# Moving elementwise work from GpSimd to VectorE in a two-layer attention kernel

## The chip, the core and the metric

The kernel runs on one core of a Trainium2 chip. A core has five engines, each with its own in-order instruction queue: TensorE (PE; its weight loads are listed as PEld), VectorE (DVE), ScalarE (ACT), GpSimd (POOL) and SyncE (SP), whose queue issues the transfers (DMAs). Engines wait for each other by semaphores. The metric is the device time of one execution in microseconds (us).

## What is computed

One step of a backbone with two layers over 256 context tokens and 1024 latent tokens, width 1024. Layer 0 mixes tokens by differential attention, layer 1 by multi-head latent attention. Each layer is a gated mixer between two normalisations, with shift, scale and gate computed from a conditioning vector. Cut to what matters here:

```
for i in range(2):
    hc = rmsnorm(x_ctx, g_pre[i]) * (1 + sc_c) + sh_c      # and hl from x_lat
    # i == 0: q, k, v, gate = h @ w_in; rope on q, k of latents; cached k, v appended
    #         w = softmax(q0 k0) - lam * softmax(q1 k1); o = w @ v per head
    #         o = rmsnorm(o, g_sub) * 0.8 * silu(gate)
    # i == 1: latent projections; k, v = c_kv @ w_kvb; o = softmax(q k) @ v * silu(gate)
    x_ctx = x_ctx + gt_c * rmsnorm(oc @ w_out[i], g_post[i])   # x_lat alike
```

Everything is float32. The outputs are both token streams and the new key/value states of the context tokens.

## The kernel before

**Products in three parts.** TensorE works on a reduced float32 form (fp32r). So each operand is kept as a high part, rounded to that form, and a low part, the operand minus its high part; a product is three matmuls, high x high, low x high, high x low (`mm3`, L327 to L329). Somebody has to make the low parts by a subtraction:

- for the weights, `weights` (L304): a piece of a weight matrix is loaded to a staging tile `wst` (three buffers, L317), ACT casts it to `wh` (L319), and L320 subtracts to `wl`. L320 runs on POOL, unless the caller hands `lo_engs`: with `self.LO` (L101) pieces alternate between POOL and DVE. This is so in the output projections (L971), layer 1's input projections (L1017, L1130) and the first head's key, query and value weights of layer 1 (L1193, L1215, L1235, with DVE first). Layer 0's value and gate weights (L499) and the later heads of layer 1 use POOL alone. A twin for rotated layouts, `weights_x` (L347), uses POOL at L365.
- for the normalised input, `norm_pair_to_hT` (L280): PE transposes a chunk (L290), ACT applies scale and shift into `hfull` (L297), DVE casts the high part `hh` (L298), and L299 makes the low part `hl`, in layer 0 by DVE for odd chunks and by POOL for even ones, in layer 1 by DVE for six of the eight (`HL`, L90).

**Tokens** are handled in five pairs of 128-token tiles, four of the latents and one of the context (`CTXP`).

**Layer 0** first computes the norms and the first value product, then query and key projections, then goes through the heads (`l0_heads`, L820). For each unit of 128 queries and one head, PE computes scores S into one of two PSUM buffers (L603), DVE takes their maxima (L605, L612, L613) and the bias (L614), ACT the exponentials (L617, L619), which frees S; DVE combines the two softmaxes (L639 to L648); PE transposes the weights (L671), ACT and DVE split them into high and low parts (L673, L674), and PE multiplies with the values (`l0_values`, L678). Between the steps of the units, a feeder (`Feeder`, L31) inserts pieces of the remaining projections, so that PE has work while the softmax chain runs. At the end of a pair, `l0_values` squares and sums the output (L701), takes the reciprocal root (`rstd`, L248: a multiply-add L251 and a power L253 on POOL), forms the row factor f (L706), scales y by it (L707) and stores y (L708).

**Gating.** `y_chunk` (L743) loads stored y and gate, multiplies them (L757), and PE transposes the product for the output projection (L768).

**Output projection** (`out_items`, L929): products per pair, squares summed by ACT (L954), small sums (L965, L966), then `residual` (L974): the root's argument (L980, DVE), the power (L983, POOL), and for either tile the scaled product (L987, DVE), its sum with x (L989, POOL), and z times the row factor plus x (L995, DVE; where z isn't scaled yet, L991 and L993). After layer 0 the result goes through `norm_pair` (L256: squares on ACT, a small sum L266, `rstd`, scaling L270) and `norm_pair_to_hT`; after layer 1 it is stored (L1692, L1693) and the kernel ends.

**Layer 1** has its projections (`l1_items`, L1042, with `row_norm` L1033 through `rstd`) and its heads (`l1_heads`, L1332), with scores (L1277 to L1281), bias (L1293), exponentials (L1295) and normalisation (L1302). L1407 and L1408 split layer 1's output again, the low part on POOL.

The order of instructions in each queue comes from a scheduler in the framework, which works from priorities and its own estimates; only the PE order of the first stage is written out by hand (L1510). A change of an engine can therefore move other instructions in the queues.

Of the kernel before, what the change touches and what calls it, by code (L numbers as in the profile page):

```python
# [12 lines left out]
ALU = mybir.AluOpType  # L13
# [4 lines left out]
P = 128  # L18
D = 1024
KC = 8  # L20
H = 8
EPS = 1e-6
# [55 lines left out]
def f32(ap):  # L78
    return ap.bitcast(F32)


class K:
# [16 lines left out]
    def __init__(self, tc, I, O):  # L99
        self.tc = tc  # L100
        self.LO = [tc.nc.gpsimd, tc.nc.vector]  # L101
        self.nc = tc.nc
        self.I = I
        self.O = O
        self.n = 0
# [142 lines left out]
    def rstd(self, pool, ss, n, width=1, tag="rs"):  # L248
        nc = self.nc
        v = self.t(pool, [P, width], tag + "v")  # L250
        nc.gpsimd.tensor_scalar(out=v, in0=ss, scalar1=1.0 / n, scalar2=EPS, op0=ALU.mult, op1=ALU.add)  # L251
        r = self.t(pool, [P, width], tag)
        nc.gpsimd.tensor_tensor(out=r, in0=v, in1=self.mhalf[:, 0:width], op=ALU.pow)  # L253
        return r

    def norm_pair(self, xs, pool, sp):  # L256

        nc = self.nc
        n = len(xs[0])
# [5 lines left out]
        if n == 2:  # L265
            nc.gpsimd.tensor_tensor(out=ss[:, 0, :], in0=ss[:, 0, :], in1=ss[:, 1, :], op=ALU.add)  # L266
        r = self.rstd(sp, ss[:, 0, :], D, 2)
# [12 lines left out]
    def norm_pair_to_hT(self, xs, l, pair, big, pool, ps, pstag):  # L280
# [4 lines left out]
        for kk in range(0, KC, 2):  # L285
# [6 lines left out]
            for j in range(2):  # L292
                k = kk + j
                a = self.ada[l][:, 1, k, cond:cond + 1]
                s = self.ada[l][:, 0, k, cond:cond + 1]
                full = self.t(pool, [P, 256], "hfull", bufs=3 - l)
                nc.scalar.activation(full, pt[:, j, :], AF.Identity, scale=a, bias=s)  # L297
                nc.vector.tensor_copy(hh[:, k, :], full)  # L298
                (nc.vector if k in (self.HL if l else (1, 3, 5, 7)) else nc.gpsimd).tensor_tensor(out=hl[:, k, :], in0=full, in1=f32(hh[:, k, :]),  # L299
                                                              op=ALU.subtract)  # L300
            yield kk


    def weights(self, W, cols, kb=2, lo_engs=None, ks=None):  # L304

# [4 lines left out]
        for k0 in range(*(ks or (0, nk)), kb):  # L310
# [8 lines left out]
            nc.scalar.copy(wh, st)  # L319
            (lo_engs or [nc.gpsimd])[k0 // kb % len(lo_engs or [0])].tensor_tensor(out=wl, in0=st, in1=f32(wh), op=ALU.subtract)  # L320
            out += [(wh[:, j, :], wl[:, j, :]) for j in range(kn)]
# [356 lines left out]
    def l0_values(self, u, rz, vh, vl, feed):  # L678
# [25 lines left out]
        for i in range(2):  # L704
            f = self.t(c.st, [P, 1], "of")
            nc.gpsimd.tensor_tensor(out=f, in0=r[:, i:i + 1], in1=rz[i], op=ALU.mult)  # L706
            nc.gpsimd.tensor_scalar(out=y[:, i, :], in0=y[:, i, :], scalar1=f, scalar2=None, op0=ALU.mult)  # L707
        nc.sync.dma_start(self.ydram[pr].rearrange("(t p) n -> p t n", p=P)[:, :, h * P:(h + 1) * P], y)  # L708
# [34 lines left out]
    def y_chunk(self, pr, kk, late=None, alt=False):  # L743
# [12 lines left out]

        nc.gpsimd.tensor_tensor(out=y, in0=y, in1=g, op=ALU.mult)  # L757
        yield 1
# [170 lines left out]
    def out_items(self, l, groups, yT, zp, pool, sp, pj, gps, after):  # L929
# [7 lines left out]
        def item(n, prs):  # L937
            def gen(ws):
                for pr in prs:
# [6 lines left out]
                    for tiles in [(0,), (1,)] if l and n == 3 and pr == NPAIR - 1 else [(0, 1)]:  # L946
# [16 lines left out]
                        if n == 2:  # L963
                            for j in (1, 2):
                                nc.gpsimd.tensor_tensor(out=ss[:, 0, :], in0=ss[:, 0, :], in1=ss[:, j, :], op=ALU.add)  # L965
                            nc.gpsimd.tensor_scalar(out=ss[:, 0, :], in0=ss[:, 0, :], scalar1=1.0 / D,  # L966
                                                    scalar2=EPS, op0=ALU.mult, op1=ALU.add)
                        after(n, pr, tiles, (zs[pr], ps, ss, gp))
                    if pr == prs[-2]:
                        yield None  # L970
            return lambda: self.weights(W, [(n * 256, 256)], lo_engs=self.LO), gen  # L971
        return [item(n, prs) for prs in groups for n in range(4)]

    def residual(self, zz, tiles, x0, xt, gp, pool, sp):  # L974
# [9 lines left out]
        for i in tiles:  # L984
# [3 lines left out]
                                           op0=ALU.mult, op1=ALU.mult)  # L988
            nc.gpsimd.tensor_tensor(out=xt[:, i, :], in0=xt[:, i, :], in1=tmp, op=ALU.add)  # L989
            if scaled is None:  # L990
                nc.vector.scalar_tensor_tensor(out=z[:, i, :], in0=z[:, i, :], scalar=ri, in1=gp[0],  # L991
                                               op0=ALU.mult, op1=ALU.mult)
                nc.gpsimd.tensor_tensor(out=z[:, i, :], in0=z[:, i, :], in1=x0[i], op=ALU.add)  # L993
            else:
# [4 lines left out]
    def l1_tok_item(self, cols, pj, evac, before):  # L999
# [4 lines left out]
        def gen(ws):  # L1004
            for pr in self.ORD1:
# [9 lines left out]
                if pr == self.ORD1[-2]:  # L1015
                    yield None
        return lambda: self.weights(W, cols, lo_engs=self.LO), gen  # L1017

# [23 lines left out]
    def l1_items(self, c1, c2, later, switch):  # L1042
# [68 lines left out]
        def gate_item(h):  # L1111
            def gen(ws):
                yield None
                for s in range(0, NPAIR, 2):
# [13 lines left out]
                    for j in range(n):  # L1128
                        nc.sync.dma_start(self.gTd[h][s + j], g[:, j, :])
            return lambda: self.weights(W, [(704 + h * P, P)], kb=4, lo_engs=self.LO), gen  # L1130

# [57 lines left out]
    def l1_kn(self, h, out):  # L1189

        nc, c, m, I = self.nc, self.c, self.m, self.I
        Wk = I["mla_w_kvb"][0].rearrange("(kc p) n -> p kc n", p=P)
        wk = self.weights(Wk, [(h * 256, P)], lo_engs=self.LO[::-1] if h == 0 else None)  # L1193
        yield 1
# [16 lines left out]
    def l1_qn(self, h, out):  # L1211

        nc, c, m, I = self.nc, self.c, self.m, self.I
        Wq = I["mla_w_qb"][0].rearrange("(kc p) n -> p kc n", p=P)
        wq = self.weights(Wq, [(h * 192, P)], lo_engs=self.LO[::-1] if h == 0 else None)  # L1215
        yield 1
# [14 lines left out]
    def l1_v(self, h, out):  # L1231

        nc, c, m, I = self.nc, self.c, self.m, self.I
        Wk = I["mla_w_kvb"][0].rearrange("(kc p) n -> p kc n", p=P)
        wv = self.weights(Wk, [((h + j) * 256 + P, P) for j in range(2)], lo_engs=self.LO[::-1] if h == 0 else None)  # L1235
        yield 1
# [513 lines left out]
```

## Time and profile before

| what | value |
|---|---|
| median of 3 runs | 1993.41 us (1992.21 to 1994.4) |
| the profiled execution, its time | 1997.65 us |
| the profiled execution, its span | 1995.8 us |
| busy: PE, DVE, ACT, POOL | 1911.7, 1248.4, 963.9, 498.9 us |
| mean granted TensorE clock | 0.989 |

The span runs from the first to the last instruction of the profiled execution. A group of instructions is named by its line in the kernel, its engine, its operation and out<-in; then come the count, the busy time, the mean duration in ns, and the idle time of the engine just before with what ended it. A line "X <- Y: total, times, longest" says that instruction X's engine stood still until Y had finished.

### The profile page before, as it was taken

How to read it: one execution, taken by the hardware profiler on the slowest of the kernel's cores; microseconds unless marked ns; L12 is line 12 of the kernel's file. 1: busy time of each engine (PE TensorE's matmuls, PEld its weight loads, DVE VectorE, ACT ScalarE, POOL GpSimd, SP SyncE). 2: the span in 40 equal slices, each digit the busy share in tenths (PEclk: the TensorE clock that was granted, in tenths of full speed). 3: DMA queues.
4: the chain of work that ended last, by engine and by line, in shares of the span. 5: the costliest groups of instructions: out<-in, count | busy, mean ns of one | idle time of the engine just before them, and what ended most of it. 6: DMA issues, size and time to landing. Idle time of an engine off the chain costs nothing.

```text
span 1995.8 us, 36154 instructions
## 1 busy us (share of the span) xinstructions
PE 1911.7 (96%) x13468; PEld 1721.9 (86%) x13468; DVE 1248.4 (63%) x2461; ACT 963.9 (48%) x2409; POOL 498.9 (25%) x693
## 2 busy tenths in 40 slices
PE   6999999999999999999998999999999999999998
PEld 5788888798989787988898999889899999998998
DVE  4644446788878786888427533446667767777413
ACT  4422123667666665666435533335445554455421
POOL 3354443213121212224334442100000000004214
PEclk9999999999999999999998999999999999999999
DMA  8555544544455454455624312442110111113412
GB/s 307 170 169 175 188 157 137 157 138 132 128 147 162 129 165 127 133 148 180 194 98 135 97 51 62 145 135 60 42 36 28 47 39 50 38 38 96 160 56 106
DMA packets 225009, 237.66 MB, mean 119 GB/s; under 512 B 25313, under 2 KB 192577, under 8 KB 224705
## 3 DMA queue, kind: packets, MB, share of 16 engines
q1 hardware_dynamic: 224672, 235.29, 38.3%
q8 instruction: 107, 1.75, 0.4%
q14 instruction: 70, 0.57, 0.1%
q10 hardware_dynamic: 160, 0.05, 0.0%
HBM read 160.48 MB, written 74.78 MB: 118 GB/s over the span
## 4 chain that ended last, share of the span: by engine, by line
PE 43%; DVE 5%; POOL 3%; ACT 2%; issue 2%; DMA 2%; SPq 0%; POOLq 0%; ACTq 0%; DVEq 0%
PE pj L327 7%; PE pj L329 7%; PE pj L328 7%; PE tp L671 3%; PE tp L327 3%; PE tp L328 3%; PE tp L329 3%; PE S L1280 1%; PE S L1281 1%; PE S L1278 1%; PE S L1279 1%; PE S L1277 1%; PE S L603 1%; DVE ptl L674 1%; DMA yst<-yTd 1%
## 5 line engine op out<-in xcount | busy, mean ns | idle before, releaser
L327 PE MATMUL pj<-wh,hh 128*128 128x256 f32 (+1 forms) x1264 | 369.4, 292 | 6.6 <-DVE ptl L674 3.5
L328 PE MATMUL pj<-wl,hh 128*128 128x256 f32 (+1 forms) x1264 | 359.1, 284 | 6.1 <-DVE wl L320 3.7
L329 PE MATMUL pj<-wh,hl 128*128 128x256 f32 (+1 forms) x1264 | 358.8, 284 | 3.4 <-POOL hl L299 1.7
L320 POOL TENSOR_TENSOR wl<-wst,wh 128x512 fp32r<-128x512 f32 (+3 forms) x95 | 110.7, 1173 | 655.1 <-ACT wh L319 608.9
L327 PEld LDWEIGHTS pj<-wh,hh 128*128 128x128 f32 x1264 | 241.7, 191 | 11.7 <-DVE ptl L674 4.1
L328 PEld LDWEIGHTS pj<-wl,hh 128*128 128x128 f32 x1264 | 242.2, 192 | 8.3 <-DVE wl L320 4.1
L329 PEld LDWEIGHTS pj<-wh,hl 128*128 128x128 f32 x1264 | 241.7, 191 | 6.5 <-POOL hl L299 3.1
L329 PE MATMUL pj<-hh,wl 128*128 128x512 f32 (+1 forms) x512 | 188.5, 368 | 1.0 <-POOL wl L365 0.9
L327 PE MATMUL pj<-hh,wh 128*128 128x512 f32 (+1 forms) x512 | 188.3, 368 | 0.0
L328 PE MATMUL pj<-hl,wh 128*128 128x512 f32 (+1 forms) x512 | 187.8, 367 | 0.0
L605 DVE TENSOR_REDUCE mA<-S 128x1 f32<-128x1024 f32 x128 | 155.4, 1219 | 46.8 <-PE S L603 45.9
L617 ACT ACTIVATE e<-S,bias 128x1024 f32<-128x1024 f32 x128 | 142.9, 1117 | 81.6 <-DVE bias L614 81.4
L603 PE MATMUL S<-kl,q 128*128 128x512 f32 x512 | 150.4, 414 | 5.5 <-ACT e L617 5.1
L673 ACT CAST pth<-tp 128x512 fp32r<-128x512 f32 (+1 forms) x208 | 98.4, 511 | 83.0 <-PE tp L671 81.9
L673 ACT CAST pth<-pj 128x512 fp32r<-128x512 f32 (+1 forms) x192 | 98.4, 519 | 73.4 <-PE pj L671 70.8
L674 DVE TENSOR_TENSOR ptl<-tp,pth 128x512 fp32r<-128x512 f32 (+1 forms) x208 | 115.1, 580 | 14.1 <-ACT pth L673 13.3
L648 DVE SCALAR_TENSOR_TENSOR e<-e,cf,e 128x512 f32<-128x512 f32 (+1 forms) x192 | 121.4, 674 | 1.1
L674 DVE TENSOR_TENSOR ptl<-pj,pth 128x512 fp32r<-128x512 f32 (+1 forms) x192 | 113.0, 592 | 12.1 <-ACT pth L673 11.5
L329 PEld LDWEIGHTS pj<-hh,wl 128*128 128x128 f32 x512 | 96.3, 188 | 20.9 <-POOL wl L365 3.9
L328 PEld LDWEIGHTS pj<-hl,wh 128*128 128x128 f32 x512 | 96.3, 188 | 16.9
L319 ACT CAST wh<-wst 128x512 fp32r<-128x512 f32 (+3 forms) x136 | 76.7, 574 | 70.1 <-issue 24.9
L603 PEld LDWEIGHTS S<-kl,q 128*128 128x128 f32 x512 | 88.8, 192 | 25.1 <-ACT e L617 8.1
(323 smaller groups left out, 5247.7 us busy)
## 6 DMA issues: line engine op xcount, KB each, us to landing
q<-qsd SPq DMA_DIRECT2D x320, 64.0 KB, 2.1
wst<-in_da_w_in_dram SPq DMA_DIRECT2D x64, 256.0 KB, 3.5
kl<-ksd SPq DMA_DIRECT2D x64, 192.0 KB, 3.7
wst<-in_w_out_dram SPq DMA_DIRECT2D x48, 256.0 KB, 2.9
ast<-in_w_ada_dram SPq DMA_DIRECT2D x8, 1024.0 KB, 6.3
wh<-in_w_ada_dram SPq DMA_DIRECT2D x32, 256.0 KB, 4.2
wl<-in_w_ada_dram SPq DMA_DIRECT2D x32, 256.0 KB, 5.1
vdh<-s SPq DMA_DIRECT2D x24, 256.0 KB, 2.1
```

The source lines that it names most:

```text
L319: nc.scalar.copy(wh, st)
L320: (lo_engs or [nc.gpsimd])[k0 // kb % len(lo_engs or [0])].tensor_tensor(out=wl, in0=st, in1=f32(wh), op=ALU.subtract)
L327: nc.tensor.matmul(out, a[0], b[0], start=first, stop=False)
L328: nc.tensor.matmul(out, a[0], b[1], start=False, stop=False)
L329: nc.tensor.matmul(out, a[1], b[0], start=False, stop=last)
L603: nc.tensor.matmul(S[:, so:so + 512], st(cc, o), kl[cc][:, so:so + 512], start=(o == 0), stop=(o == 1))
L605: nc.vector.reduce_max(out=mA[:, cc:cc + 1], in_=S, axis=AX.X)
L617: nc.scalar.activation(u.es[cc][:, 0:1024], A[cc], AF.Exp, bias=bias[:, cc:cc + 1], scale=0.125, accum_out=u.zA[:, cc:cc + 1])
L648: nc.vector.scalar_tensor_tensor(out=w[:, sl], in0=w[:, sl], scalar=cf, in1=e0[:, sl], op0=ALU.mult, op1=ALU.add)
L671: nc.tensor.transpose(tp[:, j, :], u.e[:, (c0 + j) * P:(c0 + j + 1) * P], self.ident)
L673: nc.scalar.copy(hi, tp[:, 0:cn, :])
L674: nc.vector.tensor_tensor(out=u.ptl[g][:, 0:cn, u.i * P:(u.i + 1) * P], in0=tp[:, 0:cn, :], in1=f32(hi), op=ALU.subtract)
```

## The change

VectorE does several kinds of small and middling elementwise work that GpSimd did: all low parts of weights in `weights` (the choice by `lo_engs` is gone), all low parts in `norm_pair_to_hT`, the multiply-add in `rstd` (the power stays on GpSimd), the scaling of y (two GpSimd instructions per tile become one VectorE instruction with two row factors), the gating of y, the residual additions, and the small sums of squares. `weights_x`, the rotation of q, the power, and L1408 stay on GpSimd.

```
@@ rstd
-        nc.gpsimd.tensor_scalar(out=v, in0=ss, scalar1=1.0 / n, scalar2=EPS, op0=ALU.mult, op1=ALU.add)
+        nc.vector.tensor_scalar(out=v, in0=ss, scalar1=1.0 / n, scalar2=EPS, op0=ALU.mult, op1=ALU.add)
@@ norm_pair
-            nc.gpsimd.tensor_tensor(out=ss[:, 0, :], in0=ss[:, 0, :], in1=ss[:, 1, :], op=ALU.add)
+            nc.vector.tensor_tensor(out=ss[:, 0, :], in0=ss[:, 0, :], in1=ss[:, 1, :], op=ALU.add)
@@ norm_pair_to_hT
-                (nc.vector if k in (self.HL if l else (1, 3, 5, 7)) else nc.gpsimd).tensor_tensor(out=hl[:, k, :], in0=full, in1=f32(hh[:, k, :]),
-                                                              op=ALU.subtract)
+                nc.vector.tensor_tensor(out=hl[:, k, :], in0=full, in1=f32(hh[:, k, :]), op=ALU.subtract)
@@ weights
-            (lo_engs or [nc.gpsimd])[k0 // kb % len(lo_engs or [0])].tensor_tensor(out=wl, in0=st, in1=f32(wh), op=ALU.subtract)
+            nc.vector.tensor_tensor(out=wl, in0=st, in1=f32(wh), op=ALU.subtract)
@@ l0_values
         for i in range(2):
-            f = self.t(c.st, [P, 1], "of")
-            nc.gpsimd.tensor_tensor(out=f, in0=r[:, i:i + 1], in1=rz[i], op=ALU.mult)
-            nc.gpsimd.tensor_scalar(out=y[:, i, :], in0=y[:, i, :], scalar1=f, scalar2=None, op0=ALU.mult)
+            nc.vector.tensor_scalar(out=y[:, i, :], in0=y[:, i, :], scalar1=r[:, i:i + 1], scalar2=rz[i],
+                                    op0=ALU.mult, op1=ALU.mult)
@@ y_chunk
-        nc.gpsimd.tensor_tensor(out=y, in0=y, in1=g, op=ALU.mult)
+        nc.vector.tensor_tensor(out=y, in0=y, in1=g, op=ALU.mult)
@@ out_items
-                                nc.gpsimd.tensor_tensor(out=ss[:, 0, :], in0=ss[:, 0, :], in1=ss[:, j, :], op=ALU.add)
-                            nc.gpsimd.tensor_scalar(out=ss[:, 0, :], in0=ss[:, 0, :], scalar1=1.0 / D,
+                                nc.vector.tensor_tensor(out=ss[:, 0, :], in0=ss[:, 0, :], in1=ss[:, j, :], op=ALU.add)
+                            nc.vector.tensor_scalar(out=ss[:, 0, :], in0=ss[:, 0, :], scalar1=1.0 / D,
                                                     scalar2=EPS, op0=ALU.mult, op1=ALU.add)
@@ residual
-            nc.gpsimd.tensor_tensor(out=xt[:, i, :], in0=xt[:, i, :], in1=tmp, op=ALU.add)
+            nc.vector.tensor_tensor(out=xt[:, i, :], in0=xt[:, i, :], in1=tmp, op=ALU.add)
...
-                nc.gpsimd.tensor_tensor(out=z[:, i, :], in0=z[:, i, :], in1=x0[i], op=ALU.add)
+                nc.vector.tensor_tensor(out=z[:, i, :], in0=z[:, i, :], in1=x0[i], op=ALU.add)
```

The callers of `weights` lose their `lo_engs` argument.

More of the change, by code (lines that the diff above doesn't have):

```diff
@@ L100, in __init__ @@
         self.tc = tc
-        self.LO = [tc.nc.gpsimd, tc.nc.vector]
         self.nc = tc.nc
@@ L298, in norm_pair_to_hT, with weights @@
                 nc.vector.tensor_copy(hh[:, k, :], full)
-                (nc.vector if k in (self.HL if l else (1, 3, 5, 7)) else nc.gpsimd).tensor_tensor(out=hl[:, k, :], in0=full, in1=f32(hh[:, k, :]),
-                                                              op=ALU.subtract)
+                nc.vector.tensor_tensor(out=hl[:, k, :], in0=full, in1=f32(hh[:, k, :]), op=ALU.subtract)
             yield kk
-    def weights(self, W, cols, kb=2, lo_engs=None, ks=None):
+    def weights(self, W, cols, kb=2, ks=None):
         nc, wp = self.nc, self.wp
@@ L970, in gen @@
                         yield None
-            return lambda: self.weights(W, [(n * 256, 256)], lo_engs=self.LO), gen
+            return lambda: self.weights(W, [(n * 256, 256)]), gen
         return [item(n, prs) for prs in groups for n in range(4)]
@@ L1016, in gen @@
                     yield None
-        return lambda: self.weights(W, cols, lo_engs=self.LO), gen
+        return lambda: self.weights(W, cols), gen
     def split_T(self, ps, pstag, srcs, out, nb):
@@ L1129, in gen @@
                         nc.sync.dma_start(self.gTd[h][s + j], g[:, j, :])
-            return lambda: self.weights(W, [(704 + h * P, P)], kb=4, lo_engs=self.LO), gen
+            return lambda: self.weights(W, [(704 + h * P, P)], kb=4), gen
         Wq = I["mla_w_qb"][0].rearrange("(kc p) n -> p kc n", p=P)
@@ L1192, in l1_kn @@
         Wk = I["mla_w_kvb"][0].rearrange("(kc p) n -> p kc n", p=P)
-        wk = self.weights(Wk, [(h * 256, P)], lo_engs=self.LO[::-1] if h == 0 else None)
+        wk = self.weights(Wk, [(h * 256, P)])
         yield 1
@@ L1214, in l1_qn @@
         Wq = I["mla_w_qb"][0].rearrange("(kc p) n -> p kc n", p=P)
-        wq = self.weights(Wq, [(h * 192, P)], lo_engs=self.LO[::-1] if h == 0 else None)
+        wq = self.weights(Wq, [(h * 192, P)])
         yield 1
@@ L1234, in l1_v @@
         Wk = I["mla_w_kvb"][0].rearrange("(kc p) n -> p kc n", p=P)
-        wv = self.weights(Wk, [((h + j) * 256 + P, P) for j in range(2)], lo_engs=self.LO[::-1] if h == 0 else None)
+        wv = self.weights(Wk, [((h + j) * 256 + P, P) for j in range(2)])
         yield 1
```

## The prediction

> **What bounds the kernel now.** I read the page first, then a windows view whose cuts I chose at the stages of the code: 0 to 100 us layer 0's first norms and products, 320 to 950 layer 0's attention, 950 to 1160 its output projection with residual and norm, 1350 to 1850 layer 1's attention, then the last projection. Its columns are the window, its length, and busy time (instructions) of PE, PEld, DVE, ACT, POOL.
>
> ```profile
> span 1995.8 us, 36154 instructions
> ...
> PE 1911.7 (96%) x13468; PEld 1721.9 (86%) x13468; DVE 1248.4 (63%) x2461; ACT 963.9 (48%) x2409; POOL 498.9 (25%) x693
> ...
> 0.00:100.00 100.00, 80.49 (x569) 66.18 (x570) 54.98 (x119) 42.30 (x81) 35.53 (x51) 0.97 0.72 239
> ...
> 320.00:950.00 630.00, 607.82 (x4383) 538.49 (x4382) 511.67 (x1003) 408.12 (x1068) 150.08 (x267) 0.99 0.50 147
> 950.00:1160.00 210.00, 190.82 (x1524) 182.44 (x1524) 109.03 (x194) 103.45 (x276) 86.05 (x117) 0.96 0.40 128
> ...
> 1350.00:1850.00 500.00, 492.27 (x3509) 449.54 (x3508) 357.50 (x823) 253.54 (x618) 39.53 (x49) 1.00 0.16 47
> 1850.00:1996.00 146.00, 134.35 (x1119) 132.28 (x1117) 46.95 (x83) 44.84 (x141) 40.51 (x54) 0.98 0.32 110
> ```
>
> PE is busy 96% of the span: POOL's time is nowhere the bound by itself, and emptying POOL buys only those moments in which PE waits for a chain with a POOL step in it. All PE idle time together is 1995.8 - 1911.7 = 84 us. The engine that gets the work is at 63% over the whole, but at 511.67/630 = 81% in layer 0's attention. So that stage decides, and I asked who waits for whom there (microseconds in total, times, longest):
>
> ```profile
> ACT e L617 <- DVE bias L614: 81.4, 52, 4.5
> ...
> DVE mA L605 <- PE S L603: 45.9, 43, 3.0
> DVE Z L639 <- ACT e L619: 45.7, 27, 3.4
> ...
> PEld S L603 <- ACT e L617: 8.1, 10, 3.0
> ...
> 455.42 0.14 DVE L614 SCALAR_TENSOR_TENSOR bias<-m,negl 128x2 f32<-128x2 f32 x1
> ...
> 455.60 1.12 ACT L617 ACTIVATE e<-S,bias 128x1024 f32<-128x1024 f32 x1 [1.47 <-DVE bias L614]
> ...
> 456.87 1.18 PE L603 MATMUL S<-kl,q 128*128 128x512 f32 x4
> ```
>
> There is a loop: scores S (L603), their maximum (L605, L612), the bias (L614), the exponential (L617), which frees the S buffer for the next scores. The exponential waited for DVE's bias in 52 of 64 units. In the timeline rows it ends at 455.60 + 1.12 = 456.72 and PE starts the next scores at 456.87: no slack at this place. What is put in DVE's queue ahead of L614 can reach PE.
>
> **The change part by part.** What leaves POOL, and what the same shapes cost on DVE (busy us, mean ns):
>
> ```profile
> L320 POOL TENSOR_TENSOR wl<-wst,wh 128x512 fp32r<-128x512 f32 x71 | 94.0, 1331 | 228.9 <-ACT wh L319 184.5 <-PE tp L671 44.1 <-DMA wst<-in_da_w_in_dram 0.4
> L707 POOL TENSOR_SCALAR y<-y,of 128x128 f32<-128x128 f32 x80 | 51.5, 656 | 0.0
> ...
> L253 POOL TENSOR_TENSOR ors<-orsv,mhalf 128x2 f32<-128x2 f32 x40 | 29.0, 724 | 3.3
> L299 POOL TENSOR_TENSOR hl<-hfull,hh 128x256 fp32r<-128x256 f32 x30 | 22.8, 760 | 52.6 <-DVE hh L298 52.6
> ...
> L989 POOL TENSOR_TENSOR x<-x,ztmp 128x256 f32<-128x256 f32 x10 | 14.4, 1438 | 6.0 <-DVE ztmp L987 6.0
> ...
> L1293 DVE TENSOR_SCALAR bias<-mm 128x1 f32<-128x1 f32 x80 | 11.9, 149 | 1.4
> ...
> L639 DVE TENSOR_TENSOR Z<-Z,zA 128x2 f32<-128x2 f32 x64 | 9.9, 155 | 45.7 <-ACT e L619 45.7
> ...
> L1302 DVE TENSOR_SCALAR e<-e,rz 128x256 f32<-128x256 f32 x16 | 6.3, 393 | 0.5
> ...
> L429 DVE TENSOR_TENSOR r<-r,m 128x512 f32<-128x512 f32 x8 | 5.5, 684 | 0.0
> ...
> L1167 DVE TENSOR_TENSOR qa<-qa,gTh 128x256 f32<-128x256 f32 x8 | 3.3, 416 | 0.0
> ```
>
> A subtract or multiply of 128x512 costs 0.684 us on DVE (L429, both inputs in SBUF), of 128x256 0.416 (L1167), a small sum 0.155 (L639). The scaling of y, 128x128 with two per-row factors, has no row on DVE: L1293 (one column, 0.149) and L1302 (256 columns, 0.393) bound it; 128 columns lie halfway, so I take 0.27, and the product of the two factors (L706) vanishes into it. [...]
>
> *Layer 0's attention.* Counts in the stage, by the windows view of each line (here DVE busy, POOL busy, or POOL alone):
>
> ```profile
> 320.00:950.00 630.00, 0.00 (x0) 30.91 (x24) 0.99 0.50 147
> ...
> 1350.00:1850.00 500.00, 1.40 (x2) 21.66 (x27) 1.00 0.16 47
> ...
> 320.00:950.00 630.00, 49.11 (x76) 0.99 0.50 147
> ...
> 320.00:950.00 630.00, 20.07 (x15) 0.99 0.50 147
> ```
>
> In order: L320 in this stage and in layer 1's attention, L707, L757. DVE gains 24 x 0.684 = 16.4 (weights' low parts), 76 x 0.27 = 20.5 (y), 15 x 0.684 = 10.3 (gating) and 38 x 0.155 = 5.9 (L251, one for two of L707): 53 us. Something comes back, because DVE and POOL get in each other's way:
>
> ```profile
> L614 DVE SCALAR_TENSOR_TENSOR bias<-m,negl x64: 143/151/1316, 323.4 to 949.4; 128x2 f32<-128x2 f32 x64
> ...
> L614 DVE SCALAR_TENSOR_TENSOR bias<-m,negl 128x2 f32<-128x2 f32 x64 | 14.2, 221 | 0.2
> ...
> 1046.55 1.26 POOL L320 TENSOR_TENSOR wl<-wst,wh 128x512 fp32r<-128x512 f32 x1 [0.30 <-ACT wh L319]
> ...
> 1046.58 2.05 DVE L995 SCALAR_TENSOR_TENSOR z<-z,rs,x 128x768 f32<-128x768 f32 x1
> ```
>
> L614 (minimum, median, maximum in ns) is a 0.151 us instruction that once took 1.316; against its median it loses 64 x (0.221 - 0.151) = 4.5 us. I put the three small instructions around the bias (L613, L614, L643) at three times this, 13, an estimate. DVE goes to 511.67 + 53 - 13 = 552 of 630, 88%. How much reaches PE? The quoted idle times, 45.9 in 43 waits and 45.7 in 27, are gaps of 1.3 us between busy stretches; an added instruction pushes its stretch to the next gap, about every second stretch holds a bias, and where it does, PE's slack is between nothing (the rows at 455 us) and some microseconds. Bounds: nothing of the 53 reaches PE, or all. I take a quarter of it, +13, and a third of the 13 given back, -4 (it sits on the loop itself): **+9**, from -4 to +40.
>
> *Start.* By the code 20 of the 30 L299 belong to layer 0 (four chunks of five pairs), at the start; DVE then makes both low parts of a pair in turn, 0.416 each, where POOL took 0.760 and held DVE up meanwhile. Output stage: residual and norm are chains with three or four POOL steps.
>
> ```profile
> PE xt L290 <- ACT hfull L297: 9.8, 5, 3.4
> ...
> PE pj L768 <- POOL xt L757: 3.3, 1, 3.3
> ...
> PE pj L329 <- POOL hl L299: 1.7, 6, 0.3
> ```
>
> At the start at most the 1.7 us of PE's wait and as much behind it: **-2** (0 to -4). In the output stage PE waits 3.3 once for a gated y whose chain shortens by two scalings, 2 x (0.656 - 0.27), and one gating, 20.07/15 - 0.68, so -1.4; the 9.8 hang on DVE instructions that POOL held up, as L995 at 1046.58, 2.05 us instead of the 1.01 in the tail's row below; but L320, L993 and L989 join the same DVE queue. I take a quarter, -2.6: **-4** (+3 to -9). Layer 1's attention: 27 pieces, most smaller than 128x512, about 0.4 us each (L1167's price, an estimate), 11 us on a DVE with 142 free: **+1** (0 to +5).
>
> *Tail.* It is on the path whole.
>
> ```profile
> 1990.42 1.01 DVE L995 SCALAR_TENSOR_TENSOR z<-z,rs,x 128x768 f32<-128x768 f32 x1
> ...
> 1990.58 1.43 POOL L989 TENSOR_TENSOR x<-x,ztmp 128x256 f32<-128x256 f32 x1 [0.60 <-DVE ztmp L987]
> ...
> 1992.03 0.33 SPq L1692 DMA_DIRECT2D out_dram<-x  x1
> 1992.46 0.38 SPq L1693 DMA_DIRECT2D out_dram<-z  x1
> ```
>
> POOL's add ends at 1992.01 and SP's two stores follow in order. On DVE the add takes 0.42 in place of 1.44, and the tile before finishes earlier by as much, less the 0.42 that z then waits: two tiles, **-2** (-1 to -2.5).
>
> Sum: 9 - 2 - 4 + 1 - 2 = +2 us. The profiled execution took 1997.65, span 1995.8 and 1.85 around it; the median of the runs is 1993.41, 4.2 below. I carry the difference over: 1993.41 + 2 = 1995.4.
>
> **The rivals.** *B: the gaps take it.* DVE has 118 us free in the attention stage; if the 53 fall in them, that term is -4 and the rest -7: -11, about 1982. For it: 92 us of the free time are waits with nothing to do. Against it: the loop's missing slack. [...]
>
> *C: DVE stands and waits for POOL's power.* L707 needs r, made by POOL's L253 (0.724 us), which follows L251, now on DVE: DVE, POOL, DVE. If DVE comes to L707 before r is there, all behind it stands: maxima and bias of the next unit, so ACT's exponential, so PE.
>
> ```profile
> DVE kva L1040 <- POOL rs L253: 11.2, 9, 3.9
> ```
>
> Such a round trip exists already in layer 1: 11.2/9 = 1.2 us of DVE idleness each. 38 of them at 0.8 make 30 us; with the 53, a third reaching PE, 28 - 4 - 7 = +17: about 2010. It decides where nothing else ready is queued between L251 and L707. Against it: the order in DVE's queue may put other work between.
>
> *D: the change doesn't bite*, the exchanged operations lying off the path: 1993.
>
> **How the numbers follow.** Forecast A 0.45 (own range 1988 to 2002), B 0.27, C 0.25, D 0.03. This kernel can't tell less than 0.2%, 4 us, from no change: below 1989.4 is faster, above 1997.4 slower. A spreads 0.05 faster, 0.27 same, 0.13 slower; B 0.24 faster and 0.03 same; C all slower; D same. Together 0.29, 0.33, 0.38. The range runs from B's 1982 to a little past C, 2012.
>
> **What would show it.** Right: DVE over 85% busy from 320 to 950 us, L614's maximum under 0.3 us, PE's waits for L617's exponential two or three times the 8.1 us; L995 near 1.0 us everywhere; the last store issued about 2 us sooner after the last matmul. B: those PE waits unchanged. C: DVE idle before L707 with POOL's L253 as releaser. It is wrong altogether if the low parts of weights on DVE wait long for ACT's cast (L319) inside the attention stage, a wait that POOL bore without harm (228.9 us before L320), or if the instruction order on PE comes out quite different.

## The result and the profile after

The changed kernel takes 1978.36 us (median of 6 runs, 1971.22 to 1982.36), the kernel before, on the same chip, 1993.91 (1992.21 to 1997.25). The ratio is 0.9914 with a 95% interval of 0.9894 to 0.9933: faster by 13 to 21 us, where 2 us slower was forecast and the range ended at 1982.

In the changed file a line's number is 1 to 3 smaller than before; L603 is now L601, L614 L612, L290 L289. The head of the page after, then the windows view with the cuts of the prediction:

```profile
span 1976.8 us, 35963 instructions
...
PE 1900.0 (96%) x13468; PEld 1717.2 (87%) x13468; DVE 1294.1 (65%) x2813; ACT 964.1 (49%) x2409; POOL 217.8 (11%) x261
```

```profile
320.00:950.00 630.00, 606.11 (x4411) 540.40 (x4412) 538.57 (x1164) 412.66 (x1078) 30.60 (x38) 1.00 0.51 149
950.00:1160.00 210.00, 198.24 (x1640) 190.56 (x1639) 116.96 (x284) 101.57 (x270) 19.20 (x38) 0.98 0.37 120
```

POOL gave up 281 us of work (498.9 to 217.8), and DVE took over 352 instructions and became only 46 us busier (1248.4 to 1294.1). VectorE's records can overlap in time (its two last ones of the tail, shown further down, do), and busy time counts what two of them share once; added up singly, its records grew by 78 us (1368.4 to 1446.6), still far less than the 281 that GpSimd gave up. Of the two windows PE gains in the second: from 950 to 1160 us it is busy for 198 us in place of 191 with more matmuls, and its granted clock is 0.98 in place of 0.96.

A cleaner measure of that stage is the stretch over which PE transposes z for layer 1. The view of this source line gives minimum, median and maximum duration, then the first and the last start; before, and after:

```profile
L290 PE MATMUL xt<-identr,z x60: 270/272/477, 1055.2 to 1138.3; 128*128 128x128 f32 x60
```

```profile
L289 PE MATMUL xt<-identr,z x60: 272/273/331, 1047.8 to 1122.9; 128*128 128x128 f32 x60
```

The 19.0 us between the two spans divide so: 7.4 up to the first of these transposes (1055.2 to 1047.8), 8.0 within the stretch (83.1 to 75.1), 3.6 behind it (1995.8 - 1138.3 = 857.5 to 1976.8 - 1122.9 = 853.9). The profiled execution of before was 3.7 us above its median, that of after at its own, so 15.6 of the 19 is what the medians show. What the profile of before has too much lies for the most part in the 7.4: e3_hl1, e11_sums and e13_ztmp2 below, which are no faster than before, start the stretch at 1049.7, 1051.2 and 1048.4 us. Within the stretch PE stood for 10.4 us before (83.1 - 72.7 busy, by the rows below) and stands for 4.5 after (75.1 - 70.7), 5.9 less; the other 2.1 of the 8.0 are shorter busy time at a granted clock of 0.98 in place of 0.96.

What happened within the stretch is told by the groups of DVE instructions in just that window (count, busy us, mean ns). Before:

```profile
1055.20:1138.30 83.10, 72.71 (x581) 70.47 (x580) 55.89 (x104) 45.05 (x119) 40.22 (x51) 0.96 0.38 117
...
L298 DVE CAST hh<-hfull 128x256 fp32r<-128x256 f32 x35 | 13.6, 395 | 3.9 <-ACT hfull L297 3.7
L320 DVE TENSOR_TENSOR wl<-wst,wh 128x512 fp32r<-128x512 f32 x8 | 8.3, 1051 | 3.3 <-ACT wh L319 3.3
L270 DVE TENSOR_SCALAR z<-z,rs 128x768 f32<-128x768 f32 x7 | 6.6, 975 | 0.9 <-POOL rs L253 0.9
```

After:

```profile
1047.80:1122.90 75.10, 70.65 (x582) 68.91 (x581) 57.18 (x151) 46.41 (x120) 6.00 (x9) 0.98 0.42 136
...
L318 DVE TENSOR_TENSOR wl<-wst,wh 128x512 fp32r<-128x512 f32 x16 | 10.9, 687 | 2.7 <-ACT wh L317 2.7
L297 DVE CAST hh<-hfull 128x256 fp32r<-128x256 f32 x35 | 9.8, 289 | 1.3 <-ACT hfull L296 1.2
L269 DVE TENSOR_SCALAR z<-z,rs 128x768 f32<-128x768 f32 x8 | 4.6, 617 | 0.9 <-POOL rs L252 0.9
```

DVE carries out 151 instructions in place of 104 and is busy for 57.2 us in place of 55.9: 47 more for 1.3 us. The old ones became shorter, the cast from 395 to 289 ns, the scaling of z from 975 to 617, a low part of 128x512 from 1051 to 687. Counted group by group, the added instructions take 24 us, the shorter ones give 18 back, and 4 more vanish in records that overlap. PE did the same 581 or 582 matmuls in 8 us less.

### The profile page after: what moved, and what is told of

The parts are those of the page before. It is cut to its first block, busy times and chain, and to the rows that moved or that the text cites. A ratio compares the mean times of both kernels' runs of the same rounds, so it can differ in the third digit from the quotient of the medians.

```text
span 1976.8 us, 35963 instructions
## 1 busy us (share of the span) xinstructions
PE 1900.0 (96%) x13468; PEld 1717.2 (87%) x13468; DVE 1294.1 (65%) x2813; ACT 964.1 (49%) x2409; POOL 217.8 (11%) x261
## 4 chain that ended last, share of the span: by engine, by line
PE 80%; DVE 10%; DMA 3%; ACT 3%; POOL 2%; issue 2%; SPq 0%; POOLq 0%; DVEq 0%; ACTq 0%
PE pj L325 16%; PE pj L327 15%; PE pj L326 15%; PE S L601 5%; PE tp L669 3%; PE tp L325 3%; PE tp L326 3%; PE tp L327 3%; PE pj L669 2%; DVE mA L603 2%; DVE ptl L672 2%; PE S L1275 1%; PE S L1277 1%; PE S L1278 1%; PE S L1276 1%
## 5 line engine op out<-in xcount | busy, mean ns | idle before, releaser
L603 DVE TENSOR_REDUCE mA<-S 128x1 f32<-128x1024 f32 x128 | 155.5, 1218 | 26.8 <-PE S L601 26.3
L601 PE MATMUL S<-kl,q 128*128 128x512 f32 x512 | 150.0, 413 | 4.9 <-ACT e L615 4.3
L318 DVE TENSOR_TENSOR wl<-wst,wh 128x512 fp32r<-128x512 f32 (+3 forms) x136 | 84.2, 629 | 43.4 <-ACT wh L317 41.3
L325 PEld LDWEIGHTS pj<-hh,wh 128*128 128x128 f32 x512 | 96.4, 188 | 16.4
L601 PEld LDWEIGHTS S<-kl,q 128*128 128x128 f32 x512 | 88.0, 191 | 25.2 <-ACT e L615 9.1
```

Source lines behind the costliest of these rows:

```text
L318: nc.vector.tensor_tensor(out=wl, in0=st, in1=f32(wh), op=ALU.subtract)
L325: nc.tensor.matmul(out, a[0], b[0], start=first, stop=False)
L601: nc.tensor.matmul(S[:, so:so + 512], st(cc, o), kl[cc][:, so:so + 512], start=(o == 0), stop=(o == 1))
L603: nc.vector.reduce_max(out=mA[:, cc:cc + 1], in_=S, axis=AX.X)
```

## The experiments

Theory S was that the gain arises in the stage after layer 0 (output projection, residual, norm, transposes), rival R that it comes from a relieved VectorE in the attention. "Stretch" in the table is that of the z transposes, from the same source view, and "PE stands" is the stretch less PE's busy time in just that window. Both come from one profile of each run. The stretch also holds what a lowered clock adds; kernels that change nothing in this stage range from 82.8 to 85.0 us in it (e2_att, e5_rest, e13_ztmp2), so a difference of 2 us in it may be chance. The standing time separates the kernels better. The first column names the runs, the ratio is to the kernel before on the same chip, with its 95% interval.

| run | median us | ratio | stretch us | PE stands us |
|---|---|---|---|---|
| kernel before | 1993.91 | 1 | 83.1 | 10.4 |
| changed kernel | 1978.36 | 0.9914 [0.9894, 0.9933] | 75.1 | 4.5 |
| e1_stage | 1987.35 | 0.9961 [0.9947, 0.9975] | 75.1 | 5.6 |
| e2_att | 1995.17 | 0.9999 [0.9989, 1.0010] | 82.8 | 10.2 |
| e3_hl1 | 1997.00 | 1.0009 [0.9998, 1.0020] | 82.4 | 10.7 |
| e4_shadow | 1985.19 | 0.9950 [0.9934, 0.9966] | 81.9 | 8.9 |
| e5_rest | 1992.48 | 0.9984 [0.9976, 0.9993] | 85.0 | 11.6 |
| e6_noatt | 1979.98 | 0.9923 [0.9911, 0.9936] | 75.4 | 4.8 |
| e7_wlout | 1978.61 | 0.9921 [0.9907, 0.9934] | 78.1 | 6.6 |
| e8_pre | 1971.82 | 0.9885 [0.9869, 0.9902] | 74.2 | 5.1 |
| e9_shadow2 | 1981.52 | 0.9927 [0.9908, 0.9946] | 80.6 | 9.1 |
| e10_res | 1993.21 | 0.9985 [0.9974, 0.9997] | 82.0 | 9.4 |
| e11_sums | 1997.95 | 1.0010 [0.9999, 1.0021] | 82.7 | 11.0 |
| e12_nores | 1982.87 | 0.9938 [0.9921, 0.9954] | 80.7 | 8.5 |
| e13_ztmp2 | 1994.00 | 0.9993 [0.9981, 1.0004] | 84.8 | 10.1 |
| e14_nores_z2 | 1980.09 | 0.9923 [0.9910, 0.9936] | 80.2 | 9.5 |
| e15_pre_yt | 1973.70 | 0.9894 [0.9881, 0.9907] | 76.5 | 4.6 |
| e16_stage_rn | 1983.38 | 0.9940 [0.9928, 0.9952] | 75.7 | 4.8 |

### Which place brings it

**e1_stage**: the lines of the change that belong to the stage, alone.

```
@@ norm_pair_to_hT (layer 1), weights (out_items of layer 0), norm_pair, out_items, residual (layer 0)
+                nc.vector.tensor_tensor(out=hl[:, k, :], in0=full, in1=f32(hh[:, k, :]), op=ALU.subtract)
+            nc.vector.tensor_tensor(out=wl, in0=st, in1=f32(wh), op=ALU.subtract)
+            nc.vector.tensor_tensor(out=ss[:, 0, :], in0=ss[:, 0, :], in1=ss[:, 1, :], op=ALU.add)
+            nc.vector.tensor_tensor(out=xt[:, i, :], in0=xt[:, i, :], in1=tmp, op=ALU.add)
+                nc.vector.tensor_tensor(out=z[:, i, :], in0=z[:, i, :], in1=x0[i], op=ALU.add)
...
```

> The kernel before, with VectorE doing only what belongs to the output projection, residual and norm after layer 0 (low parts of the output weights, layer 1's low parts of h, small sums, the multiply-add in the norm's rstd, residual additions); attention as before. Theory S (the gain comes from this stage: TensorE stood still there for chains with GpSimd steps, and its clock was halved after each long stop): 1977 to 1983 us, the clock in 950-1160 at least 0.98. Rival R (the gain comes from relief of VectorE in the attention stage): 1989 to 1994. The prediction's terms (stage -4): 1989.

**e2_att**: the lines that belong to layer 0's attention, alone.

```
@@ rstd (from l0_values), weights (from l0_tok_item), l0_values, y_chunk
+            nc.vector.tensor_scalar(out=y[:, i, :], in0=y[:, i, :], scalar1=r[:, i:i + 1], scalar2=rz[i],
+                                    op0=ALU.mult, op1=ALU.mult)
+        nc.vector.tensor_tensor(out=y, in0=y, in1=g, op=ALU.mult)
...
```

> The kernel before, with VectorE doing only what belongs to layer 0's attention: low parts of the value and gate weights, rstd's multiply-add there, scaling and gating of y. Theory S: 1988 to 1995. Rival R: 1978 to 1985. The prediction's terms (attention +9): 1999 to 2003.

**e6_noatt**: the reverse, the changed kernel with the lines of e2_att back on GpSimd.

> The changed kernel with the attention parts of e2_att back on GpSimd (low parts of the value and gate weights, rstd's multiply-add in layer 0's heads, scaling and gating of y). If the parts add up: 1977 to 1981, like the changed kernel, since e2_att gave nothing alone. If the attention parts bring the missing -9 in company: 1985 to 1989.

**e5_rest**: the lines that are in neither: layer 0's `hl`, the first value product's and layer 1's weights, layer 1's row norms, the last projection.

> The kernel before, with VectorE doing only what belongs neither to the stage of e1_stage nor to the attention of e2_att: the first value product's low parts, layer 0's low parts of h, layer 1's weights and row norms, the last projection. If the parts add up, this brings what e1_stage (-8) and e2_att (0) leave of the -17: 1985 to 1989. If the gain needs the parts together: 1992 to 1996.

The stage alone brings 8 us (0.9961), less than S expected in time, and the whole 8 us of the stretch (75.1). The attention brings nothing, alone (0.9999) or in company: without it 0.9923 is left of 0.9914, inside the interval. R falls. The rest brings 3 us (0.9984), where 1985 to 1989 us was expected if the parts add up. The three alone sum to 11 us, the whole gives 17 by its ratio. The four intervals together leave this difference of 6 us an uncertainty of 5.5, so little or nothing need be missing; e16_stage_rn below looks for it.

### What in the stage

**e3_hl1**: ten subtractions (`hl` of two chunks) alone.

```
@@ norm_pair_to_hT
-                (nc.vector if k in (self.HL if l else (1, 3, 5, 7)) else nc.gpsimd).tensor_tensor(
+                (nc.vector if l or k % 2 else nc.gpsimd).tensor_tensor(
```

> The kernel before, with only layer 1's low parts of h all on VectorE (10 instructions of 80 change engine). ScalarE's hfull has two buffers there and waited 13.5 us in nine waits for GpSimd's hl. If that is the chain behind TensorE's waits for hfull: 1986 to 1989; if it is only one of several links: 1991 to 1994.

**e10_res** and **e11_sums**: the residual additions alone, the small sums alone. (Theory X, here and later: GpSimd's reading slows VectorE, and that is what the stage cost. Theory W: it was the round trips VectorE, GpSimd, VectorE in the residual.)

> The kernel before, with only the residual additions of the stage (L989, L993) on VectorE. Theory W: most of e1_stage's gain, 1986 to 1990. Theory X: a third of it or less, 1991 to 1996.

> The kernel before, with only the small sums of the stage on VectorE (L965, L966, L266 and the norm's L251, each under 0.25 us on GpSimd). Theories W and X alike: within 3 us of before, 1992 to 1997. If the hops between engines in front of these sums are what cost: 1987 to 1991.

None does it alone: PE stands for 10.7, 9.4 and 11.0 us against 10.4, and the ratios are 1.0009, 0.9985 and 1.0010. The stage's fourth part, the low parts of the output weights, was not tried alone. Two parts were taken out of the changed kernel instead, with the weights (**e7_wlout**) or the additions (**e12_nores**) back on GpSimd:

> The changed kernel with one part of the stage undone: the low parts of the output projections' weights alternate between GpSimd and VectorE again. If the reading of these 128x512 instructions beside VectorE's long ones is what cost the stage: 3 to 8 us slower than the changed kernel, 1981 to 1986, and the stretch between the last two output products and the first transpose for layer 1 back at 9 us from 6. If the residual additions and layer 1's hl cost it: 1977 to 1980.

> The changed kernel with only the stage's residual additions back on GpSimd. Theory W: 1983 to 1987. Theory X: 1978 to 1981, since two thirds of GpSimd's reading time in the stage stays away.

Undone singly, both parts cost stretch, 3.0 us (78.1) and 5.6 us (80.7), of which 2.2 and 4.1 are standing time of PE. In time neither is clear of the changed kernel: e7_wlout's 0.9921 is the same, and the interval of e12_nores (0.9938, some 5 us slower, between what X and W expected) still overlaps that of 0.9914. The reading that fits both series is that several GpSimd parts held the same waits of TensorE, and taking one away left the next.

### Reading beside, or the instructions themselves

**e4_shadow** leaves all work with VectorE and lets GpSimd do the old amount beside it, for nobody:

```
@@ weights (out_items of layer 0, every second piece)
+                for j in range(kn):
+                    nc.gpsimd.tensor_tensor(out=self.shadow, in0=f32(wl[:, j, :]), in1=f32(wh[:, j, :]), op=ALU.subtract)
@@ norm_pair_to_hT (layer 1, chunks 0 and 4)
+                    nc.gpsimd.tensor_tensor(out=self.shadow, in0=f32(hl[:, k, :]), in1=f32(hh[:, k, :]), op=ALU.subtract)
@@ residual (layer 0)
+                nc.gpsimd.tensor_tensor(out=self.shadow, in0=xt[:, i, :], in1=tmp, op=ALU.add)
```

> The changed kernel, in which GpSimd also does an instruction of the old shape and length after each of those it did in the stage (half of the output weights' low parts, layer 1's hl of two chunks, the residual sum), into a scratch tile that nobody reads; nothing but GpSimd's own powers stands behind them. If VectorE lost its time by GpSimd's reading beside it (contention): half of the stage's gain or more is lost, 1984 to 1991, and L992 is again seen at 1.4 us and more. If the time was in the length and queue of the old instructions themselves: 1977 to 1981, with at most a microsecond for the powers.

1985.19, with 0.0036 of the 0.0086 gone, which is within what contention was to give, an interval just clear of the changed kernel's, and a stretch of 81.9. But its third part makes VectorE's own sum wait until the shadow has read xt (0.64, 0.91 and 0.62 us between 1035 and 1048 us). **e9_shadow2** drops that part:

> The shadow of e4_shadow without its part at the residual sum (there VectorE's own sum waited for the shadow, 0.6 to 0.9 us each): GpSimd repeats only half of the output weights' low parts and layer 1's hl of two chunks, reading finished tiles, so that VectorE waits for nothing of it but powers queued behind. Theory X (GpSimd's reading slows VectorE, and that is what the stage cost): 1982 to 1987. Theory W (it was the round trips VectorE, GpSimd, VectorE in the residual, with one ztmp buffer): 1977 to 1981.

In the stretch of e9_shadow2, by the same three views (its line numbers are 4 to 11 higher than before's):

```profile
L294 PE MATMUL xt<-identr,z x60: 270/272/332, 1043.7 to 1124.3; 128*128 128x128 f32 x60
...
1043.70:1124.30 80.60, 71.51 (x582) 69.10 (x581) 65.04 (x150) 46.13 (x120) 24.53 (x31) 0.98 0.39 127
...
L303 DVE TENSOR_TENSOR hl<-hfull,hh 128x256 fp32r<-128x256 f32 x34 | 17.1, 520 | 0.3
L302 DVE CAST hh<-hfull 128x256 fp32r<-128x256 f32 x35 | 12.2, 363 | 0.9 <-ACT hfull L301 0.7
L326 DVE TENSOR_TENSOR wl<-wst,wh 128x512 fp32r<-128x512 f32 x16 | 11.9, 751 | 2.6 <-ACT wh L325 2.6
```

18.5 us of GpSimd work that nobody uses (24.53 - 6.00) made VectorE 7.9 us busier with as many instructions (65.04 against 57.18) and the stretch 5.5 us longer. The powers queued behind it were not late: VectorE's waits for them add up to 6.2 us in the stretch, against 6.0 in the changed kernel and 9.8 before. PE stands for 9.1 us, so GpSimd's presence alone brings back 4.6 of the 5.9 us that the change had saved. The casts went from 289 ns in the changed kernel to 363, the low parts of h from 421 to 520, those of the weights from 687 to 751; the scaling of z stayed at 615, and the mark named for e4_shadow, the residual's z at 1.4 us, came in neither run. In time it is less sure: 1981.52 lies between the two ranges, 0.9927 [0.9908, 0.9946] is 3 us above the changed kernel, and the intervals overlap.

**e13_ztmp2** and **e14_nores_z2** tried the rest, a round trip: with one `ztmp` buffer VectorE's second product waits for GpSimd's first sum (1.9 us in three waits in the stage before).

```
@@ residual (layer 0), in the kernel before and in e12_nores
-            tmp = self.t(pool, [P, 256], "ztmp")
+            tmp = self.t(pool, [P, 256], "ztmp", bufs=2)
```

> The kernel before with two ztmp buffers in the stage's residual instead of one; TensorE's order is unchanged. VectorE waited 0.63 us three times there for GpSimd's sum (L989) to free it. If this round trip held the stage: 1990 to 1993 and the stretch between the last two output products and layer 1's first transpose shorter than 9 us. If GpSimd's reading and the length of its sums held it: within 2 us of before.

> e12_nores (the changed kernel, residual additions back on GpSimd, +4.5 us) with two ztmp buffers. If the round trip through ztmp was the +4.5: 1977 to 1980. If GpSimd's sum itself was, by its length or its reading: 1981 to 1985.

e13_ztmp2 shows nothing (0.9993, PE stands for 10.1 us). e14_nores_z2 came out at the edge of what the round trip was to give, 3 us below e12_nores with overlapping intervals, but PE stood no less in its stretch, 9.5 us after 8.5. So by the profiles the buffer isn't what held the stage; the additions' own length and reading remain, and in time this stays open.

### Where the parts don't add up

**e16_stage_rn**: e1_stage with one more line, the multiply-add of layer 1's row norms (`rstd` from `row_norm`).

> e1_stage with the multiply-add of layer 1's row norms on VectorE as well. In e1_stage TensorE still stopped at 1138 and 1139 us behind this instruction on GpSimd, and its clock was halved there. If the missing us lie at this seam: 1982 to 1985, and no halving near 1150 us. If not: 1986 to 1989.

0.9940 against 0.9961 is 4 us, as expected for the seam, but the intervals overlap from 0.9947 to 0.9952, and the profiles don't put the gain there. The same stretch of PE's work behind the last transpose of z, some 567 matmuls, in e1_stage, e16_stage_rn and e5_rest (PE's busy time stands first behind the length, the granted clock third from the right):

```profile
1124.00:1193.00 69.00, 66.14 (x568) 65.61 (x567) 24.59 (x53) 25.18 (x63) 25.70 (x58) 0.98 0.15 41
```

```profile
1125.40:1192.90 67.50, 64.62 (x568) 64.09 (x567) 25.69 (x65) 25.18 (x63) 20.86 (x46) 1.00 0.16 42
```

```profile
1136.50:1202.10 65.60, 64.34 (x567) 63.96 (x566) 27.04 (x69) 25.31 (x64) 16.86 (x43) 1.00 0.16 43
```

With the row norm's instruction moved PE stands as long as without it, 2.9 us; what is gone is the lowered clock, 0.98 in e1_stage over these 69 us, and the kernel before didn't have it here either (67.4 us, clock 1.00). In e5_rest, and in the changed kernel, PE stands for 1.3 and 1.2 us here: the stop that is gone waited for another GpSimd instruction, `kps` (L1072 before), 1.5 us in e16_stage_rn. Of e5_rest's lines only layer 1's weights and the row norms run here, so by elimination it is the weights that held `kps` up: some 1.6 us of standing at the seam, and for the row norm nothing that the profiles show.

### A late load, and a faster version

In the changed kernel the attention lost time at one place that the kernel before doesn't have. Its timeline, on SP's queue, ACT and PE, and the same load before:

```profile
420.76 2.86 SPq L509 DMA_DIRECT2D s<-in_cache_diff_v_dram  x1
...
430.38 0.62 ACT L502 CAST s<-s 128x512 fp32r<-128x512 f32 x1 [3.40 <-DMA s<-in_cache_diff_v_dram]
430.90 1.11 ACT L615 ACTIVATE e<-S,bias 128x1024 f32<-128x1024 f32 x1
...
432.16 1.52 PE L601 MATMUL S<-kl,q 128*128 128x512 f32 x4 [3.21 <-ACT e L615]
```

```profile
415.86 1.66 SPq L511 DMA_DIRECT2D s<-in_cache_diff_v_dram  x1
...
419.96 0.62 ACT L504 CAST s<-s 128x512 fp32r<-128x512 f32 x1 [0.23 <-DMA s<-in_cache_diff_v_dram]
```

SP now issues the load of cached values behind two other loads, 4.9 us later; ACT's cast stands ahead of the exponential and waits 3.40 us for it, and PE 3.21 behind that; the granted clock is 0.50 from 433 to 436 us. **e8_pre** issues the load one pair of tokens earlier than the cast:

```
@@ l0_tok_item
-                if kind == "v" and pr == 1:
-                    self.l0_cached_v(hp)
+                if kind == "v" and pr == 0:
+                    cr = self.l0_load_cached_v(hp)
+                if kind == "v" and pr == 1:
+                    self.l0_split_v(hp, cr, 8)
```

> The changed kernel, with the load of cached values issued one token pair earlier than its cast. In the changed kernel ScalarE and VectorE stood 3.4 us for this load at 427 us, TensorE 3.5 us behind them, and its clock was halved for another 3.4. If that late load is what layer 0's heads 1 to 5 lost (5 to 7 us): 1971 to 1975, and scores of head 2 start near 475 us. If another wait takes its place: 1977 to 1980.

1971.82 us, ratio 0.9885 [0.9869, 0.9902]: the fastest here, 6 us below the changed kernel by the two ratios, though the intervals overlap by 0.0008. ACT's 8.2 us of waits for such loads in the attention are gone from its trace; 4.2 of them stood in the kernel before as well, so this is more than an undoing of the change's harm. By the slope given at the end, 3 of the 6 us are what its higher mean clock makes (0.9938 against 0.9913), of which chance may be a part.

**e15_pre_yt** moved the next GpSimd line, the low part of layer 1's output (L1408), on top of it:

> e8_pre with the low part of layer 1's output (yT, the only line of GpSimd left beside layer 1's last head) on VectorE as well. TensorE stood some 7 us in five stops between 1785 and 1835 us in e8_pre, twice within 0.3 us after this line's end. If VectorE lost time beside it: 1967 to 1970. If VectorE, busy there, now holds the softmax up: 1972 to 1977.

0.9894, no gain and no loss that can be told.

## Why the prediction was wrong

**Layer 0's attention, +9: the sign.** What was added is about what was counted, 57 us of busy time, 60 added up singly (after, the attention's window):

```profile
L703 DVE TENSOR_SCALAR y<-y,ors,rz 128x128 f32<-128x128 f32 x60 | 18.6, 344 | 10.9 <-POOL ors L252 10.9
L318 DVE TENSOR_TENSOR wl<-wst,wh 128x512 fp32r<-128x512 f32 x24 | 16.0, 684 | 0.4 <-ACT wh L317 0.4
L754 DVE TENSOR_TENSOR kl<-kl 128x512 f32<-128x512 f32 x10 | 6.8, 685 | 1.7 <-DMA kl<-g 1.7
L250 DVE TENSOR_SCALAR orsv<-oss 128x2 f32<-128x2 f32 x38 | 6.2, 163 | 0.0
L703 DVE TENSOR_SCALAR y<-y,ors,rzx 128x128 f32<-128x128 f32 x16 | 4.9, 343 | 0.7 <-POOL ors L252 0.7
L754 DVE TENSOR_TENSOR wst<-wst,wst 128x512 f32<-128x512 f32 x7 | 4.8, 684 | 0.1
```

DVE's busy time rose by only 26.9 (511.67 to 538.57), but not because the relief was larger than the 13 us that the forecast took for three small instructions. Their rows before (the bias L614 has its row in the prediction) and after give 12:

```profile
L643 DVE SCALAR_TENSOR_TENSOR cf<-Z,neglam,rz 128x1 f32<-128x1 f32 x62 | 16.9, 273 | 1.1 <-DVE rz L641 0.2
L613 DVE TENSOR_TENSOR m<-m,mA 128x2 f32<-128x2 f32 x64 | 13.9, 218 | 0.1
```

```profile
L641 DVE SCALAR_TENSOR_TENSOR cf<-Z,neglam,rz 128x1 f32<-128x1 f32 x63 | 13.6, 216 | 1.0
L612 DVE SCALAR_TENSOR_TENSOR bias<-m,negl 128x2 f32<-128x2 f32 x64 | 9.9, 155 | 0.1
L611 DVE TENSOR_TENSOR m<-m,mA 128x2 f32<-128x2 f32 x64 | 9.7, 151 | 0.1
```

Other instructions give back some 7 more. The rest is the overlap of records: added up singly they grew by 44.5 us (571.4 to 616.0), and 17.6 of that lies in time that two records share. So three signs of the forecast came true: DVE is 85.5% busy, the bias never takes longer than 0.163 us, and z's L992 stays between 1.007 and 1.019. The step that failed is the share that reaches PE, "I take a quarter of it": nearly nothing did.

```profile
ACT e L615 <- DVE bias L612: 81.3, 49, 5.4
...
DVE Z L637 <- ACT e L617: 34.3, 22, 3.4
DVE mA L603 <- PE S L601: 26.3, 31, 2.6
...
DVE y L703 <- POOL ors L252: 11.7, 23, 0.9
...
PEld S L601 <- ACT e L615: 9.1, 13, 3.4
```

The exponential waits for the bias as before, PEld for the exponential 9.1 us and not two or three times 8.1, and one stop of that is the late load; with PE's own waits it is 13.4 after 13.2. What DVE gained in work it lost in idleness: its waits for Z and S fell from 45.7 and 45.9 to 34.3 and 26.3. That is rival B's "the gaps take it" for this stage. The order of PE's instructions did come out different, which the forecast named as a sign against it: at 1494 of the 13468 places another instruction stands, and e2_att's lines alone do this at 1199, without a change in time. e2_att puts the term at 0 (2 us either way). C's mechanism was there too, DVE standing before L703 for POOL's power, but for 0.5 us a time (11.7/23), and PE didn't feel it.

**Output stage, -4: the size, and two of its steps.** "I take a quarter" of PE's 9.8 us of waits for hfull was the step (that is 2.45; the forecast has 2.6). After, this wait is 4.3, so 5.5 us went:

```profile
PE xt L289 <- ACT hfull L296: 4.3, 4, 2.7
```

The stretch alone gave 8 in the profile, the stage alone 8 in time. The one long z (2.05 us) was taken for the case; the rows show the cast at 1.4, the scaling of z at 1.6 and the weights' low parts at 1.5 times their length. Their shares in PE's waits can't be told singly, as the runs with one part alone show. Left out entirely was the clock: around the 3.29 us stop for the late `wl` of before, its granted value (third number from the right) was 0.57 over 8 us, and 0.50 in each of the six microseconds from 1048 on. How much of such a halving belongs to the kernel and how much to chance isn't known from one profile.

```profile
1047.00:1055.00 8.00, 5.71 (x28) 5.72 (x29) 5.12 (x9) 3.55 (x11) 3.10 (x6) 0.57 0.72 229
```

GpSimd's work beside VectorE's was given too small a price: in e9_shadow2 18.5 us of it made VectorE 7.9 us busier.

**Start, -2: too large.** The first scores start at 317.9 us after 318.1 in the profile. **Layer 1, +1, and tail, -2: together -3.6** behind the stretch. The tail gave little of it. Last PE instruction, the two last DVE instructions and the last store's issue, after, and the last PE instruction before:

```profile
1967.54 0.28 PE L327 MATMUL pj<-wh,yT 128*128 128x256 f32 x1
...
1971.20 1.01 DVE L992 SCALAR_TENSOR_TENSOR z<-z,rs,x 128x768 f32<-128x768 f32 x1
1972.12 0.42 DVE L986 TENSOR_TENSOR x<-x,ztmp 128x256 f32<-128x256 f32 x1
...
1972.96 0.42 SPq L1690 DMA_DIRECT2D out_dram<-z  x1
```

```profile
1985.88 0.27 PE L329 MATMUL pj<-wh,yT 128*128 128x256 f32 x1
```

From there to the last store 5.4 us in place of 6.6 (1992.46 - 1985.88): 1.2 sooner, since x's sum now waits behind z's 1.01 on the same engine. Some 1.6 us are at the seam to layer 1, which the forecast didn't name.

**Rivals.** B had the right mechanism in the attention and, at 1982, the nearest time; its -4 in the output stage was as short as the forecast's. C and D fell.

## What to carry to other kernels

Where two engines slow each other, the one that takes over work gets something back: look stage by stage how far the means of its large groups stand above the minimum of the same shape. That excess is what a move can give back; here it paid for 18 of 24 us of added work in the stretch of the z transposes, and for 19 of 60 in layer 0's attention. Weigh the stages by where TensorE stops, not by how busy the receiving engine is. Test parts by taking them out of the new kernel as well as putting them into the old one: where several parts hold the same wait, one alone can show nothing. And compare the time that TensorE stands in a stage, not only the stage's length: it keeps the chance of the clock out.

## What the runs showed of the hardware

**What GpSimd slows.** Two rows of before, of DVE and POOL: an instruction with one input from PSUM ran its 0.68 us beside GpSimd's subtraction unharmed. The six of this line in the stretch have a mean of 684 ns before and 686 after.

```profile
1075.60 0.68 DVE L960 TENSOR_TENSOR z<-pj,gp 128x512 f32<-128x512 f32 x1
...
1075.55 0.73 POOL L299 TENSOR_TENSOR hl<-hfull,hh 128x256 fp32r<-128x256 f32 x1 [1.29 <-DVE hh L298]
```

The casts and the scalings of z, each with one SBUF input, were slowed, 395 against 289 ns and 975 against 617 in the mean. Singly, in the kernel before: a cast took 1.93 us from 1059.13 beside GpSimd's sum of z (L993, 1.82 us from 1059.09), and 0.29 at 1062.27 with GpSimd idle; a scaling took 2.19 beside another of these sums (2.14 us from 1054.50), and 0.62 at 1071.96 with GpSimd idle.

**What the clock did after a stop.** The first transposes after three like stops, each with the window behind it (the third number from the right is the granted clock): the changed kernel, e8_pre, e1_stage.

```profile
1114.35 0.66 PE L289 MATMUL xt<-identr,xt 128*128 128x128 f32 x4 [2.67 <-ACT hfull L296]
...
1114.00:1118.00 4.00, 3.65 (x22) 3.66 (x23) 2.92 (x11) 1.71 (x5) 0.86 (x2) 0.69 0.00 0
```

```profile
1108.29 0.66 PE L294 MATMUL xt<-identr,xt 128*128 128x128 f32 x4 [2.69 <-ACT hfull L301]
...
1108.00:1112.00 4.00, 3.71 (x32) 3.71 (x33) 2.98 (x11) 1.67 (x6) 0.81 (x2) 1.00 0.01 2
```

```profile
1116.79 0.66 PE L294 MATMUL xt<-identr,xt 128*128 128x128 f32 x4 [2.90 <-ACT hfull L301]
...
1116.00:1121.00 5.00, 4.21 (x36) 4.21 (x37) 4.04 (x13) 3.39 (x8) 0.74 (x2) 1.00 0.00 0
```

A stop of 2.67 us was followed by a clock of 0.69 over 4 us (22 matmuls), stops of 2.69 and 2.90 by a full clock (in e8_pre 32 matmuls in as long). In the kernel before the four stops of 2.77 to 3.38 us between 950 and 1160 us were each followed by 2 us or more at a clock of 0.50, the one of 2.35 us by a full clock. So the length of a stop alone doesn't tell whether the clock falls behind it, and what else does is not shown. The clock is much of what the runs differ by: over the 78 runs of the kernel before that were made beside the experiments, time fell by 1.28 us for each 0.001 of mean granted clock (correlation -0.77). By that slope the mean clocks, 0.9898 before and 0.9913 after, account for 2 of the 16 us. The clock also bounds what single profiles tell: a difference of 1 to 3 us between two of them may be one halving (an estimate: 0.69 over 4 us lacks 1.2 us of full clock, 0.57 over 8 us lacks 3.4).

**Two factors are dearer than one.** The scaling of y with two per-row factors took 343 ns for 128 columns, where 270 was taken from one-factor rows. The changed kernel's scalings with one factor (L269) take medians of 348, 616 and 750 ns for 256, 768 and 1024 columns; on that line 128 columns would take 281, an estimate, so the second factor costs about 60 ns here.
